# One hybrid decoder layer in a single instruction plan: norms kept per token, sums left in DRAM, another order of products and a plain opening of the first down projection

## The chip, the core and the metric

The kernel runs on one core of a Trainium2 chip. The metric is the device time of one execution in microseconds (us). A core has TensorE (PE, matmul, with a separate weight load PEld), VectorE (DVE), ScalarE (ACT), GpSimd (POOL) and SyncE (SP, which here only issues transfers), an on-chip SBUF of 128 partitions and a PSUM of eight banks, 128 x 512 fp32 each, into which PE writes.

## The reference

One layer on `x` of 1024 tokens by 1024 columns, and a last norm:

```python
def rms_norm(x, g):
    return x * lax.rsqrt(jnp.mean(x * x, -1, keepdims=True) + EPS) * g

mod = silu(c) @ mod_w + mod_b                      # 9 vectors of 1024
u = modulate(rms_norm(x, norm1_g), sh1, sc1)
x = x + 0.5 * g1 * swiglu(u, ffn1_w_up, ffn1_w_down)      # d_ff = 2816
u = modulate(rms_norm(x, norm2_g), sh2, sc2)
xa, ga, xb, mg_a, mg_b = split(u @ w_in + b_in)
ya = rg_lru(causal_depthwise_conv(xa)) * gelu(ga)
yb = gelu(s5_ssm(xb)); yb = yb * sigmoid(yb @ glu_w + glu_b)
m = sigmoid(mg_a) * (ya @ proj_a) + sigmoid(mg_b) * (yb @ proj_b)
x = x + g2 * (m @ w_out)
u = modulate(rms_norm(x, norm3_g), sh3, sc3)
x = x + 0.5 * g3 * swiglu(u, ffn2_w_up, ffn2_w_down)
out = rms_norm(x, final_g)
```

## The kernel before

Activations lie transposed: a tile has 128 columns of the model on its partitions and 512 tokens (half h = 0 or 1) along its rows, so x is 8 x 2 tiles. All arithmetic is fp32. A product of a 128 x 128 weight block with a tile is three matmuls in the chip's rounded fp32 form: weight and operand are each split into a rounded part (ACT, names `wh`, `act`) and a remainder (DVE, `wl`, `act`), and hi x hi, hi x lo and lo x hi are summed in a PSUM bank (`products`).

Two ways of multiplying are used. The *plain* way (`tile_of`) takes one output tile for both halves, k by k. The *paired* way (`pair`, `pair_weights`, `pair_operands*`) takes two output tiles, two halves and two halves of k as a 2 x 2 block problem and does it with seven products instead of eight, numbered 1 to 7. The weights of the products are sums of weight blocks, made by accumulating transfers that POOL issues (`plus`); the operands are sums and differences of tiles on DVE, each split again. Products 1, 2 and 3 use tiles of B as they are; 4 to 7 use sums. `pair_operands` makes them block by block of k, `pair_operands_by_product` in the order in which `pair` wants them (1, 6, 2, 7, 5, 4, 3). After products, `pair` adds banks together: a copy on ACT (`s1`) and six additions on DVE.

Nothing is issued as it is written. Every call is recorded in a `Plan`, which then sets the order on each engine: it walks a clock of its own with costs from `cost`, and takes on each engine the ready call of lowest number. `ahead` lowers the number (weights by 200, sums of pairs by 300, loads of gated tiles by 100). A tile needs a free slot of its tag (65 of `act`, 6 `tmp`, 8 `wh`, 8 `wl`, 4 `wr`, 8 banks); a call whose slot isn't free waits. All instructions therefore have one line (L437 before, L439 after), and tiles are told by name. Background work (modulation vectors, the set-up of S5, the scans) is spread between products by `spread` and `tick` at a rate per tick.

The order of the work: norm of x; up projection of FFN1 with SwiGLU, gated tiles to DRAM (`g_d`); its down projection in four blocks of k (6, 6, 6 and 4 tiles of 128), each plain or paired as `PARTS` says, the outputs being summed in 16 SBUF tiles of x; norm; `w_in`: S5 input first (`put_xb`, four plain tiles), then the gates ga and mg_a paired, then xa and mg_b plain, with S5 and the scans in the background; `proj_b`, `proj_a` (four pairs), `w_out`; norm; FFN2 in the same way, with its sums kept in DRAM; last norm in three pieces (512, 256 and 256 tokens).

A norm sums squares over columns, so over partitions: squares on ACT, added over the 8 tiles on DVE (or in PSUM, in the first norms), then a matmul with a 128 x 128 block of ones, which leaves the sum of each token in all 128 rows; square root on ACT, reciprocal on DVE, 128 x 512 each.

Of the kernel before, what the change touches and what calls it, by code (L numbers as in the profile page):

```python
# [46 lines left out]
SETUP_RATE, MOD_RATE, GAIN_RATE, LATE_RATE = 1.0, 0.18, 0.1, 0.2  # L47
# [7 lines left out]
    ((6, True), (6, False), (6, True), (4, False)),  # L55
# [18 lines left out]
class Plan:  # L74
# [130 lines left out]
    def cost(self, call, table):  # L205
        engine, method, args, kwargs = call
        out = args[0]
        n = 1
        for s in out.shape[1:]:
            n *= s  # L210
        psum = any(
            getattr(a, "space", None) == bass.MemoryType.PSUM for a in args[1:]
        )
        if engine == "tensor":
            rhs = kwargs.get("rhs", args[1] if len(args) > 1 else None)
            return max(60.0, n * 1.7 if rhs.dtype == F32 else (n + 32) / 2.4), table
# [13 lines left out]
        return 65 + n * (max(rate, 1.05) if psum else rate), table  # L230
# [211 lines left out]
class Layer:  # L442
# [175 lines left out]
    def pair_operands_by_product(self, b11, b21, b12, b22):  # L618

        nc = self.nc  # L620
        split = lambda ts: [self.split(t) for t in ts]
        xs = {1: split(b11)}
# [7 lines left out]
        xs[2] = split(b21)  # L630
# [7 lines left out]
        xs[3] = split(b22)  # L638
        return xs

    def pair(self, w, xs):
# [13 lines left out]
        self.tick()  # L655
        product(b, 6)
# [3 lines left out]
        product(a, 2, True)  # L660
        self.tick()
# [12 lines left out]
        product(c, 3, True)  # L674
# [29 lines left out]
    def square(self, st, x, d):  # L704
# [5 lines left out]
        if st[0] is None:  # L710
            st[0] = sq
        else:
            acc = self.act()[:, :n]
            nc.two(ALU.add, acc, st[0], sq)
            st[0] = acc

    def rstd(self, st):

        nc = self.nc
        n = st[0].shape[1]  # L720
        hi, lo = self.tmp(F32R)[:, :n], self.tmp(F32R)[:, :n]
        nc.scalar.activation(hi, st[0], AF.Copy)
        nc.vector.tensor_sub(lo, st[0], hi.bitcast(F32))
        ps = self.bank()[:, :n]
        self.mm(ps, self.ones, hi, True, False)
        self.mm(ps, self.ones, lo, False, True)
        return self.rstd_of(ps)

    def rstd_of(self, ps):
        nc = self.nc  # L730
        n = ps.shape[1]
        root = self.tmp()[:, :n]
        nc.scalar.activation(root, ps, AF.Sqrt, bias=self.eps, scale=1.0 / D)
        r = self.act()[:, :n]
        nc.vector.reciprocal(r, root)
        return r

    def modulate(self, x, r, l, d):

        nc = self.nc  # L740
        if r is not None:
            nc.two(ALU.mult, x, x, r)
# [58 lines left out]
    def up(self, w_up, u, t, f0, job=None):  # L801

        xs = self.pair_operands(
# [213 lines left out]
def s5_setup(L):  # L1017
# [5 lines left out]
    L.ident = L.con("ident", [P, P])  # L1023
    st = {}

    def params():
        softplus_scales(L)
        yield
        make_identity(L.tc.nc, L.ident)
# [217 lines left out]
class Mixer:  # L1247
# [19 lines left out]
    def put_xb(self, m, h, ps):  # L1267
# [4 lines left out]
            t.rearrange("p (j c) -> p c j", j=4), ps.rearrange("p (c j) -> p c j", j=4),  # L1272
# [222 lines left out]
    def run(self):  # L1495
# [4 lines left out]
        xs = L.pair_operands(  # L1500
# [7 lines left out]
        for dst, i0, fn in ((self.ga_d, 8, AF.Gelu_apprx_tanh), (self.mga_d, 20, AF.Sigmoid)):  # L1508
            for i in range(i0, i0 + 8, 2):
                c11, c12, c21, c22 = L.pair(  # L1510
                    L.pair_weights([io["w_in"][i], io["w_in"][i + 1]]), xs
# [38 lines left out]
        for p, pair in enumerate(PROJ_A):  # L1550
            c11, c12, c21, c22 = L.pair(L.pair_weights([io["proj_a"][d] for d in pair]), ya)
            for e, h, c in ((0, 0, c11), (1, 1, c22), (1, 0, c21), (0, 1, c12)):
                d = pair[e]
                t, r = self.load(self.mga_d, d, h), self.load(self.q_d, d, h)
                nc.vector.tensor_mul(t, t, c)
                nc.two(ALU.add, t, t, r)
                if p < M_OUT:
                    nc.sync.dma_start(self.m_d[d][:, h * H : (h + 1) * H], t)
                    with nc.ahead(GATED_AHEAD):
                        m[h][d] = self.load(self.m_d, d, h)  # L1560
                else:
                    m[h][d] = t
# [5 lines left out]
        st = [[None], [None]]  # L1568
        u3 = L.u3 = [[], []]

        def put(d, h, ps):
# [4 lines left out]
            L.square(st[h], t, d)  # L1576
            x[h][d] = self.load(L.x2_d, d, h) if d < W_PAIRED else t
            if d == ND - 1:
                s = L.rstd(st[h])
# [41 lines left out]
def hybrid_layer(ctx: ExitStack, tc: tile.TileContext, io):  # L1621
# [6 lines left out]
    L.ones = L.con("ones", [P, P], F32R)  # L1628
# [3 lines left out]
    nc.vector.memset(L.ones.bitcast(F32), 1.0)  # L1632
# [37 lines left out]
    def norm(h):  # L1670
        ps = L.bank()
        for d in range(ND):
            sq = L.act()
            nc.scalar.activation(sq, x[h][d], AF.Square)
            L.mm(ps, L.ones.bitcast(F32), sq, d == 0, d == ND - 1)
        r = L.rstd_of(ps)
        for d in range(ND):
            nc.two(ALU.mult, x[h][d], x[h][d], r)
# [48 lines left out]
    st = [[None], [None]]  # L1727
    u2 = [[], []]

    def on_x(d, h, x):  # L1730
        L.square(st[h], x[h][d], d)
        if d == ND - 1:
            r = L.rstd(st[h])
# [13 lines left out]
    st3 = [[None] for _ in pieces]  # L1747

    def on_out(d, p, x):
        h, c = pieces[p]  # L1750
        L.square(st3[p], x[h][d][:, c], d)
        if d == ND - 1:
# [4 lines left out]
            r = L.rstd(st3[p])  # L1757
            for e in range(ND):
                if e in scaled:
                    o = scaled[e]  # L1760
                    nc.gpsimd.tensor_mul(o, o, r)
# [109 lines left out]
```

## Time and profile before

| | |
|---|---|
| time, median of 3 runs | 2054.34 us (2054.18 to 2054.97) |
| the profiled execution | 2057.46 us, of which 2055.7 us are the span of the profile |
| PE busy | 1991.2 us, 97% of the span, 8866 matmul rows |
| DVE busy | 1554.1 us, 76% |
| ACT busy | 1065.2 us, 52% |
| POOL busy | 324.3 us, 16% |
| mean granted clock of TensorE | 0.987 of full speed |
| transfers | 393.06 MB, mean 191 GB/s |

The busy share is an average over stages. Rows of the views give start, duration, engine, line, operation, tile written <- tiles read, shape; a row of the timeline with x3 at its end stands for three instructions in a row, and the bracket says how long the engine had been idle before it, and what ended that. Matmul rows overlap, so distances between starts say more than durations.

### The profile page before, as it was taken

Reading aid. Unit: us, or ns where it says so; the run is one execution under the profiler, and the core shown is the slowest. Engines: PE = TensorE matmul, PEld = TensorE weight load, DVE = VectorE, ACT = ScalarE, POOL = GpSimd, SP = SyncE. Lnnn points to the kernel's source line nnn. Section 1 sums busy time; section 2 is a strip of 40 time slices with the busy share of each in tenths; the row PEclk is TensorE's granted clock in tenths of the full one; section 3 lists DMA queues with packets and bytes.
Section 4 is the critical chain, followed back from the end, with each engine's and each line's share of the span. In section 5 each row is a group of like instructions: output and inputs, shape, how many; then the busy total and the mean of one; then the engine's idle time right before and its main releaser. Section 6 shows DMA issues by size and latency. Waiting matters only on the chain. (4 is left out here: it accounts for less than half of the span.)

```text
span 2055.7 us, 27034 instructions
## 1 busy us (share of the span) xinstructions
PE 1991.2 (97%) x8866; PEld 1635.7 (80%) x8866; DVE 1554.1 (76%) x3064; ACT 1065.2 (52%) x1842; POOL 324.3 (16%) x409
## 2 busy tenths in 40 slices
PE   6999999998999999999999999899999999999997
PEld 3888888886888878788878888677888888887886
DVE  8997777778969787767999597879544444497757
ACT  5744344344434574455789643447443344366753
POOL 0222122121011001100000011100111121134442
PEclk9999999999999999999999999999999999999998
DMA  7767676778756367787555689662765565589993
GB/s 261 192 156 208 180 197 185 198 193 265 238 156 178 130 172 206 217 251 248 174 173 196 230 253 280 210 235 74 173 159 133 129 150 136 123 210 220 203 230 127
DMA packets 188045, 393.06 MB, mean 191 GB/s; under 512 B 20992, under 2 KB 44672, under 8 KB 187904
## 3 DMA queue, kind: packets, MB, share of 16 engines
q1 hardware_dynamic: 121504, 278.45, 40.8%
q0 software_dynamic: 49536, 84.96, 24.6%
q10 hardware_dynamic: 16864, 27.93, 3.7%
q8 instruction: 69, 1.13, 0.2%
q14 instruction: 72, 0.59, 0.1%
HBM read 262.81 MB, written 92.27 MB: 173 GB/s over the span
## 5 line engine op out<-in xcount | busy, mean ns | idle before, releaser
L437 PE MATMUL ps_in<-act_in,wh_in 128*128 128x512 f32 (+1 forms) x5592 | 1685.6, 390 | 37.3 <-ACT act_in L437 12.5
L437 PEld LDWEIGHTS ps_in<-act_in,wh_in 128*128 128x128 f32 x5592 | 1050.0, 189 | 263.5 <-DVE act_in L437 17.2
L437 PE MATMUL ps_in<-act_in,wl_in 128*128 128x512 f32 (+1 forms) x2796 | 1047.7, 389 | 0.0
L437 ACT ACTIVATE wh_in<-wr_in 128x512 fp32r<-128x512 f32 (+2 forms) x544 | 323.8, 601 | 571.6 <-PE ps_in L437 451.7
L437 PEld LDWEIGHTS ps_in<-act_in,wl_in 128*128 128x128 f32 x2796 | 528.6, 189 | 107.6
L437 DVE TENSOR_TENSOR wl_in<-wr_in,wh_in 128x512 fp32r<-128x512 f32 (+2 forms) x544 | 352.3, 653 | 174.3 <-ACT wh_in L437 173.1
L437 DVE TENSOR_TENSOR act_in<-act_in,act_in 128x512 f32<-128x512 f32 (+3 forms) x632 | 400.0, 677 | 30.9 <-ACT act_in L437 24.0
L437 DVE TENSOR_TENSOR tmp_in<-ps_in,tmp_in 128x512 f32<-128x512 f32 x296 | 203.9, 689 | 160.3 <-PE ps_in L437 157.0
L437 ACT ACTIVATE act_in<-act_in 128x512 fp32r<-128x512 f32 (+3 forms) x414 | 238.0, 612 | 129.6 <-DVE act_in L437 107.0
L437 POOL DMA_DIRECT2D wr_in<-wr_in x148 | 136.5, 922 | 544.9 <-ACT wr_in L437 169.8
L437 ACT ACTIVATE tmp_in<-ps_in 128x512 f32<-128x512 f32 x130 | 76.3, 589 | 51.9 <-PE ps_in L437 44.2
L437 POOL DMA_DIRECT2D re_in<-in_ffn_w_up x40 | 35.6, 890 | 426.0 <-ACT re_in L437 307.0
L437 ACT ACTIVATE wr_in<-wr_in 128x512 f32<-128x512 f32 (+1 forms) x148 | 85.2, 594 | 23.3 <-DVE wl_in L437 21.9
L437 DVE TENSOR_TENSOR tmp_in<-tmp_in,ps_in 128x512 f32<-128x512 f32 x82 | 56.0, 685 | 41.7 <-PE ps_in L437 41.1
L437 ACT ACTIVATE wh_in<-re_in 128x512 fp32r<-128x512 f32 (+1 forms) x74 | 44.3, 599 | 67.9 <-PE ps_in L437 65.2
L437 DVE SCALAR_TENSOR_TENSOR mw_in<-mw_in,cact 128x1024 f32<-128x1024 f32 x56 | 68.3, 1220 | 8.3 <-DMA mw_in<-in_mod_w 8.2
L437 DVE TENSOR_TENSOR tmp_in<-tmp_in,tmp_in 128x512 f32<-128x512 f32 (+1 forms) x96 | 66.0, 688 | 5.8 <-ACT tmp_in L437 5.2
L437 DVE SCALAR_TENSOR_TENSOR act_in<-ps_in,mods,act_in 128x512 f32<-128x512 f32 (+1 forms) x68 | 46.2, 686 | 29.1 <-PE ps_in L437 28.9
L437 PE MATMUL ps_in<-act_in,act_in 128*128 128x256 f32 (+1 forms) x336 | 57.8, 317 | 3.8 <-DVE act_in L437 2.3
L437 PEld LDWEIGHTS ps_in<-act_in,act_in 128*128 128x128 f32 x336 | 49.2, 190 | 12.5 <-DVE act_in L437 4.9
L437 POOL DMA_DIRECT2D x_d<-tmp_in x48 | 50.2, 1266 | 53.0 <-ACT tmp_in L437 51.5
L437 ACT ACT_TABLE_LOAD x42 | 53.9, 1283 | 2.4 <-PEq L1860 1.7
(109 smaller groups left out, 1019.4 us busy)
## 6 DMA issues: line engine op xcount, KB each, us to landing
wr_in<-in_ffn_w_up SPq DMA_DIRECT2D x84, 512.0 KB, 3.7
mw_in<-in_mod_w SPq DMA_DIRECT2D x56, 512.0 KB, 4.3
wr_in<-wr_in POOLq DMA_DIRECT2D x108, 256.0 KB, 5.1
g_d<-tmp_in SPq DMA_DIRECT2D x88, 256.0 KB, 4.0
act_in<-g_d SPq DMA_DIRECT2D x88, 256.0 KB, 6.0
wr_in<-in_ffn_w_down SPq DMA_DIRECT2D x48, 384.0 KB, 4.0
wr_in<-in_w_in SPq DMA_DIRECT2D x36, 512.0 KB, 3.9
x_d<-tmp_in POOLq DMA_DIRECT2D x48, 256.0 KB, 7.5
```

The source lines that it names most:

```text
L437: getattr(getattr(self.nc, engine), method)(*map(self.place, args), **{k: self.place(v) for k, v in kwargs.items()})
```

## The change

Seven edits, all in what is recorded; the order of everything is then set anew by the planner.

1. The two first norms and the three pieces of the last one keep the sum of a token on the token's own partition. For the last norm the squares are the weights of matmuls with two columns of ones (`square`), so that four (or two) blocks of 128 tokens give a tile of 128 x 8 (128 x 4); for the first norms the full sums are copied out of PSUM and brought into this form by four matmuls with two columns of an identity. Square root and reciprocal work on 128 x 8, and four (two) fp32 matmuls with the identity spread the result over 128 rows again, into PSUM, from where the multiplications read it (`rstd`). A square root of 128 x 2 at the first square of a piece (`early`) is there to set ACT's table. The norms of FFN1's output and of w_out's keep the old form (`rstd_rows`).
2. For the first two pairs of `proj_a` the gated product is added to `q_d` in DRAM by an accumulating transfer and read back, instead of being added on DVE, stored to `m_d` and read back.
3. In the first pair of gates the products go 1, 3, 2, 6, 7, 5, 4, with product 3 in a fifth bank and one more addition.
4. `up` (FFN1, FFN2) and the gates make their operands by product.
5. `put_xb` reads PSUM strided and writes in order, instead of the reverse.
6. FFN1's down projection is plain, paired, paired, plain instead of paired, plain, paired, plain.
7. Two background rates are lower, and the planner's cost of short fp32 matmuls is higher; the identity is made at the start.

The diff, cut to its core:

```diff
-SETUP_RATE, MOD_RATE, GAIN_RATE, LATE_RATE = 1.0, 0.18, 0.1, 0.2
+SETUP_RATE, MOD_RATE, GAIN_RATE, LATE_RATE = 1.0, 0.14, 0.1, 0.16
 PARTS = (
-    ((6, True), (6, False), (6, True), (4, False)),
+    ((6, False), (6, True), (6, True), (4, False)),
     ((6, True), (6, True), (6, True), (4, False)),
 )
-    def pair(self, w, xs):
+    def pair(self, w, xs, late=False):
...
+        if late:
+            e = self.bank()
+            product(e, 3)
+            product(a, 2, True)
+            self.tick()
         product(b, 6)
         with nc.ahead(SUMS_AHEAD):
             nc.vector.tensor_add(u2, b, s1)
         self.tick()
-        product(a, 2, True)
-        self.tick()
+        if late:
+            with nc.ahead(SUMS_AHEAD):
+                nc.vector.tensor_add(u2, e, u2)
+        else:
+            product(a, 2, True)
+            self.tick()
...
+    def rstd(self, ps, n):
+
+        nc = self.nc
+        k = n // P
+        r = self.con(self.name("rstd"), [P, 2 * k])
+        self.root(r, ps[:, : 2 * k])
+        nc.vector.reciprocal(r, r)
+        out = self.bank()[:, :n]
+        for b in range(k):
+            self.mm(
+                out[:, b * P : (b + 1) * P], r[:, 2 * b : 2 * b + 1].to_broadcast([P, P]),
+                self.ident, True, True,
+            )
+        return out
...
     def up(self, w_up, u, t, f0, job=None):
 
-        xs = self.pair_operands(
+        xs = self.pair_operands_by_product(
...
         nc.scalar.activation(
-            t.rearrange("p (j c) -> p c j", j=4), ps.rearrange("p (c j) -> p c j", j=4),
+            t.rearrange("p (j c) -> p j c", j=4), ps.rearrange("p (c j) -> p j c", j=4),
             AF.Identity, bias=L.col("b_in", 16 + m),
         )
...
-                t, r = self.load(self.mga_d, d, h), self.load(self.q_d, d, h)
+                t = self.load(self.mga_d, d, h)
                 nc.vector.tensor_mul(t, t, c)
-                nc.two(ALU.add, t, t, r)
                 if p < M_OUT:
-                    nc.sync.dma_start(self.m_d[d][:, h * H : (h + 1) * H], t)
+                    nc.plus(self.q_d[d][:, h * H : (h + 1) * H], t)
                     with nc.ahead(GATED_AHEAD):
-                        m[h][d] = self.load(self.m_d, d, h)
+                        m[h][d] = self.load(self.q_d, d, h)
                 else:
+                    r = self.load(self.q_d, d, h)
+                    nc.two(ALU.add, t, t, r)
                     m[h][d] = t
...
-        r = L.rstd_of(ps)
+        sums = L.tmp()
+        nc.scalar.activation(sums, ps, AF.Copy)
+        ps = L.bank()
+        for b in range(H // P):
+            L.mm(
+                ps[:, 2 * b : 2 * b + 2], sums[:, b * P : (b + 1) * P], L.ident[:, :2],
+                True, True,
+            )
+        r = L.rstd(ps, H)
         for d in range(ND):
-            nc.two(ALU.mult, x[h][d], x[h][d], r)
+            nc.vector.tensor_mul(x[h][d], x[h][d], r)
```

How the order moves, at three places. First PE where FFN1's down projection opens, before (product 1 of the paired block into `ps_983`, then product 6 into `ps_984`, which the order leaves after two of its three blocks of k):

```order
L437 MATMUL ps_983_in<-act_922_in,wh_969_in 128x512
L437 MATMUL ps_983_in<-act_923_in,wh_969_in 128x512
L437 MATMUL ps_983_in<-act_922_in,wl_970_in 128x512
L437 MATMUL ps_984_in<-act_930_in,wh_973_in 128x512
L437 MATMUL ps_984_in<-act_931_in,wh_973_in 128x512
L437 MATMUL ps_984_in<-act_930_in,wl_974_in 128x512
```

and the same place now (the last rows of the up projection, in `ps_896`, then the first plain tile, both halves of it in `ps_950` and `ps_951`):

```order
L439 MATMUL ps_896_in<-act_207_in,wh_892_in 128x512
L439 MATMUL ps_896_in<-act_206_in,wl_893_in 128x512
L439 MATMUL ps_950_in<-act_910_in,wh_946_in 128x512
L439 MATMUL ps_950_in<-act_911_in,wh_946_in 128x512
L439 MATMUL ps_951_in<-act_913_in,wh_946_in 128x512
L439 MATMUL ps_951_in<-act_914_in,wh_946_in 128x512
L439 MATMUL ps_950_in<-act_910_in,wl_947_in 128x512
```

Before, the block that opens is paired; now it is plain, and its first k is followed by the next k in the same two banks.

Second, DVE at the step from the second to the third block of FFN1's down projection, which are both paired now (the first row is the last sum of the second block; the `act` rows with `act` inputs are differences, or remainders of operands, of the third; `wl` are remainders of weights; the rows of act_1198, act_1200 and act_1202 are the remainders that product 6 waits for, those of act_1204, act_1206 and act_1208 those of product 2; `tmp_1255` is a sum after the third block's first product 6):

```order
L439 TENSOR_TENSOR tmp_1171_in<-ps_1168_in,tmp_1171_in 128x512
L439 TENSOR_TENSOR act_1196_in<-act_1193_in,act_1184_in 128x512
L439 TENSOR_TENSOR act_1198_in<-act_1194_in,act_1197_in 128x512
L439 TENSOR_TENSOR act_1200_in<-act_1195_in,act_1199_in 128x512
L439 TENSOR_TENSOR wl_1261_in<-wr_1257_in,wh_1260_in 128x384
L439 TENSOR_TENSOR act_1202_in<-act_1196_in,act_1201_in 128x512
L439 TENSOR_TENSOR act_1204_in<-act_1176_in,act_1203_in 128x512
L439 TENSOR_TENSOR wl_1249_in<-wr_1233_in,wh_1248_in 128x384
L439 TENSOR_TENSOR wl_1263_in<-wr_1257_in,wh_1262_in 128x384
L439 TENSOR_TENSOR tmp_1255_in<-ps_1251_in,tmp_1254_in 128x512
L439 TENSOR_TENSOR act_1206_in<-act_1177_in,act_1205_in 128x512
L439 TENSOR_TENSOR act_1208_in<-act_1178_in,act_1207_in 128x512
```

Before, a plain block stood between two paired ones; there is no such place in the order of before.

Third, DVE in the first norms, before (a remainder of the first operand, two modulation vectors, then the reciprocal of the second half and its first multiplications):

```order
L437 TENSOR_TENSOR act_131_in<-act_72_in,act_130_in 128x512
L437 SCALAR_TENSOR_TENSOR wr_132_in,mods<-wr_132_in,cact 128x1024
L437 SCALAR_TENSOR_TENSOR wr_133_in,mods<-wr_133_in,cact 128x1024
L437 TENSOR_TENSOR mods<-mods,cols 128x1
L437 RECIPROCAL act_146_in<-tmp_145_in 128x512
L437 SCALAR_TENSOR_TENSOR gsc<-mods,cols 128x1
L437 TENSOR_TENSOR mods<-mods,cols 128x1
L437 TENSOR_TENSOR act_122_in<-act_122_in,act_146_in 128x512
```

and now (the same remainder, the modulation vectors, then remainders of weights):

```order
L439 TENSOR_TENSOR act_138_in<-act_77_in,act_137_in 128x512
L439 SCALAR_TENSOR_TENSOR wr_139_in,mods<-wr_139_in,cact 128x1024
L439 SCALAR_TENSOR_TENSOR wr_140_in,mods<-wr_140_in,cact 128x1024
L439 TENSOR_TENSOR mods<-mods,cols 128x1
L439 TENSOR_TENSOR wl_95_in<-act_156_in,wh_94_in 128x256
L439 SCALAR_TENSOR_TENSOR gsc<-mods,cols 128x1
L439 TENSOR_TENSOR mods<-mods,cols 128x1
L439 TENSOR_TENSOR wl_99_in<-act_157_in,wh_98_in 128x256
L439 TENSOR_TENSOR wl_103_in<-act_158_in,wh_102_in 128x256
L439 TENSOR_TENSOR wl_107_in<-act_159_in,wh_106_in 128x256
L439 TENSOR_TENSOR wl_97_in<-act_178_in,wh_96_in 128x256
```

The reciprocal of the second half (128 x 8 now) stands 24 rows behind that remainder instead of four, after twelve remainders of weights and two more modulation vectors, and its eight multiplications follow three rows later.

## Rows read from the trace of the kernel before

**Rows 1.** The profile's page: span, busy time by engine, granted clock in 40 slices

```profile
span 2055.7 us, 27034 instructions
...
PE 1991.2 (97%) x8866; PEld 1635.7 (80%) x8866; DVE 1554.1 (76%) x3064; ACT 1065.2 (52%) x1842; POOL 324.3 (16%) x409
...
PEclk9999999999999999999999999999999999999998
```

**Rows 2.** Windows: length, then busy time of each engine (instructions), PEclk, DMA share, GB/s

```profile
480.00:510.00 30.00, 21.55 (x82) 16.44 (x82) 24.68 (x56) 9.39 (x20) 6.15 (x7) 0.83 0.98 295
...
510.00:520.00 10.00, 10.00 (x45) 8.10 (x44) 9.82 (x19) 4.16 (x9) 0.52 (x1) 1.00 0.26 67
...
750.00:770.00 20.00, 16.27 (x61) 12.93 (x60) 17.47 (x29) 15.64 (x26) 2.65 (x3) 0.83 0.84 255
...
1290.00:1320.00 30.00, 22.88 (x87) 17.26 (x86) 24.46 (x45) 9.93 (x17) 3.08 (x4) 0.89 0.61 194
...
1380.00:1400.00 20.00, 17.09 (x68) 13.49 (x67) 17.40 (x25) 16.00 (x26) 1.73 (x2) 0.91 0.42 132
```

**Rows 3.** Timelines, FFN1's down opening: PE, then ACT, then PE's short S5 rows

```profile
493.09 0.50 PE L437 MATMUL ps_in<-act_in,wh_in 128*128 128x512 f32 x1 [3.16 <-ACT act_in L437]
...
503.10 1.22 PE L437 MATMUL ps_in<-act_in,wh_in 128*128 128x512 f32 x2 [3.50 <-DVE tmp_in L437]
...
491.99 0.52 ACT L437 ACTIVATE wh_in<-wr_in 128x384 fp32r<-128x384 f32 x1 [5.81 <-DMA wr_in<-wr_in]
...
498.62 0.98 PE L437 MATMUL ps_in<-cb_in,act_in 128*128 128x32 f32 x8
```

**Rows 4.** Timeline of DVE, splits of m ahead of w_out

```profile
1298.91 5.50 DVE L437 TENSOR_TENSOR act_in<-act_in,act_in 128x512 fp32r<-128x512 f32 x9
```

**Rows 5.** Timelines, first gates: ACT (S5 input, copy of the sum), then PE

```profile
739.73 1.20 ACT L437 ACTIVATE tmp_in<-ps_in,cols 128x512 f32<-128x512 f32 x1
...
764.12 0.58 ACT L437 ACTIVATE tmp_in<-ps_in 128x512 f32<-128x512 f32 x1
...
764.75 1.22 PE L437 MATMUL ps_in<-act_in,wh_in 128*128 128x512 f32 x2 [3.73 <-ACT tmp_in L437]
```

**Rows 6.** Timelines, norm ahead of FFN2: DVE, PE, then ACT

```profile
1383.61 3.35 DVE L437 RECIPROCAL act_in<-tmp_in 128x512 f32<-128x512 f32 x1
...
1386.87 1.23 DVE L437 TENSOR_TENSOR wl_in<-wr_in,wh_in 128x512 fp32r<-128x512 f32 x2
...
1390.83 0.49 PE L437 MATMUL ps_in<-act_in,wh_in 128*128 128x512 f32 x1 [2.47 <-ACT act_in L437]
...
1380.35 1.28 ACT L437 ACT_TABLE_LOAD   x1
1381.64 0.69 ACT L437 ACTIVATE tmp_in<-ps_in,eps 128x512 f32<-128x512 f32 x1
```

**Rows 7.** Timelines, first norms: DVE, ACT, PE

```profile
18.86 3.35 DVE L437 RECIPROCAL act_in<-tmp_in 128x512 f32<-128x512 f32 x1
...
22.25 5.51 DVE L437 TENSOR_TENSOR act_in<-act_in,act_in 128x512 f32<-128x512 f32 x9
...
13.43 1.28 ACT L437 ACT_TABLE_LOAD   x1
...
35.59 0.79 PE L437 MATMUL ps_in<-act_in,wh_in 128*128 128x512 f32 x1 [5.00 <-ACT act_in L437]
```

**Rows 8.** Timelines, the end: PE, DVE

```profile
2045.89 0.58 PE L437 MATMUL ps_in<-tmp_in,ones 128*128 128x256 f32 x1 [0.42 <-DVE tmp_in L437]
...
2047.08 1.75 DVE L437 RECIPROCAL act_in<-tmp_in 128x256 f32<-128x256 f32 x1 [1.24 <-ACT tmp_in L437]
...
2048.87 3.56 DVE L437 SCALAR_TENSOR_TENSOR act_in<-act_in,cols,act_in 128x256 f32<-128x256 f32 x5
```

**Rows 9.** Groups of DVE by form, whole span: sums from PSUM, sums from SBUF

```profile
L437 DVE TENSOR_TENSOR tmp_in<-ps_in,tmp_in 128x512 f32<-128x512 f32 x296 | 203.9, 689 | 160.3 <-PE ps_in L437 157.0 <-DMA ga_d<-tmp_in 1.1 <-DMA x_d<-tmp_in 0.7
...
L437 DVE TENSOR_TENSOR act_in<-act_in,act_in 128x512 f32<-128x512 f32 x280 | 182.8, 686 | 17.0 <-ACT act_in L437 11.1 <-DMA act_in<-q_d 4.2 <-DMA act_in<-g_d 1.1
```

More of the change, by code (lines that the diff above doesn't have):

```diff
@@ L629, in pair_operands_by_product @@
         xs[6] = split(t2)
-        xs[2] = split(b21)
+        if not known:
+            xs[2] = split(b21)
         for r, v in zip(b12, b22):
@@ L673, in pair @@
         self.tick()
-        product(c, 3, True)
+        if not late:
+            product(c, 3, True)
         with nc.ahead(SUMS_AHEAD):
@@ L709, in square @@
         nc.scalar.activation(sq, x, AF.Square)
-        if st[0] is None:
-            st[0] = sq
-        else:
+        if d == 0:
+            st[:] = [sq, None]
+            self.root(self.con(self.name("early"), [P, 2]), sq[:, :2])
+            return
+        if rows or d < ND - 1:
             acc = self.act()[:, :n]
@@ L715, in square @@
             st[0] = acc
-    def rstd(self, st):
+        if rows:
+            return
+        if d == ND - 2:
+            hi, lo = self.tmp(F32R)[:, :n], self.tmp(F32R)[:, :n]
+            nc.scalar.activation(hi, acc, AF.Copy)
+            nc.vector.tensor_sub(lo, acc, hi.bitcast(F32))
+            st[1] = self.bank()
+            for b in range(n // P):
+                c = slice(b * P, (b + 1) * P)
+                out = st[1][:, 2 * b : 2 * b + 2]
+                self.mm(out, hi[:, c], self.ones, b == 0, False, b > 0)
+                self.mm(out, lo[:, c], self.ones, False, True, b > 0)
@@ L719, in rstd, with root, rstd_rows @@
+        if d == ND - 1:
+            for b in range(n // P):
+                self.mm(
+                    st[1][:, 2 * b : 2 * b + 2], sq[:, b * P : (b + 1) * P],
+                    self.ones.bitcast(F32), False, True, True,
+                )
+    def root(self, out, sums):
+        self.nc.scalar.activation(out, sums, AF.Sqrt, bias=self.eps, scale=1.0 / D)
+    def rstd_rows(self, st):
         nc = self.nc
-        n = st[0].shape[1]
-        hi, lo = self.tmp(F32R)[:, :n], self.tmp(F32R)[:, :n]
+        hi, lo = self.tmp(F32R), self.tmp(F32R)
@@ L722, in rstd @@
         nc.scalar.activation(hi, st[0], AF.Copy)
         nc.vector.tensor_sub(lo, st[0], hi.bitcast(F32))
[L724 to L734, printed above, removed]
+        ps = self.bank()
@@ L735, in rstd_of @@
+        self.mm(ps, self.ones_p, hi, True, False)
+        self.mm(ps, self.ones_p, lo, False, True)
+        root = self.tmp()
+        self.root(root, ps)
+        r = self.act()
         nc.vector.reciprocal(r, root)
         return r
+    def rstd(self, ps, n):
[6 more added lines that the diff above has]
+        for b in range(k):
+            self.mm(
+                out[:, b * P : (b + 1) * P], r[:, 2 * b : 2 * b + 1].to_broadcast([P, P]),
+                self.ident, True, True,
+            )
+        return out
@@ L1627, in hybrid_layer @@
     L.gsc = L.con("gsc", [P, 24])
-    L.ones = L.con("ones", [P, P], F32R)
+    L.ones_p = L.con("ones_p", [P, P], F32R)
+    ones = L.ones_p.bitcast(F32)
+    L.ones = L.ones_p[:, :2]
+    L.ident = L.con("ident", [P, P])
+    make_identity(tc.nc, L.ident)
     L.eps = L.con("eps", [P, 1])
@@ L1756, in on_out @@
                 nc.scalar.activation(scaled[e], x[h][e][:, c], AF.Copy, scale=L.col("final_g", e))
-            r = L.rstd(st3[p])
+            r = L.rstd(st3[p][1], c.stop - c.start)
+            if scaled:
+                r_copy = L.act()[:, : c.stop - c.start]
+                nc.scalar.activation(r_copy, r, AF.Copy)
             for e in range(ND):
```

44 lines of the change are left out of this document (24 added, 20 removed).

## Prediction, made before the changed kernel was run

> **What bounds the kernel now.** The page comes first: PE is busy for 1991.2 us of a span of 2055.7 us, and the granted clock is 9 tenths or more in 39 of 40 slices [rows 1]. No other engine comes near, so the time is the products plus the places where PE stands still or runs slowly. The change leaves the number of products as it is; what it can win are those places, about 65 us in all, and the windows say where they are [rows 2]. A full stretch of 10 us holds 45 matmul rows (510 to 520 us). By that measure 480 to 510 us has 82 rows, of which 12 are short ones of S5 that take 1.3 us, so 30 - 70/4.5 - 1.3 = 13 us are lost; 750 to 770 us loses 20 - 61/4.5 = 6.4; 1290 to 1320 us loses 30 - 87/4.5 = 10.7; 1380 to 1400 us loses 20 - 68/4.5 = 4.9. [...] The reader then asks the timelines what PE waited for in each. Besides these four there are the start and the end, where 9 us of the span lie behind the last matmul row (2045.89 + 0.58) [rows 8].
>
> **1. FFN1's down opens plain.** PE waits 3.16 us for ACT and 3.50 us for DVE there, and ACT itself stood 5.81 us on an accumulating transfer of weights [rows 3], with the DMA engines at 0.98 [rows 2]. A paired opening needs seven sums of operands and POOL's sums of weights at once; a plain one needs twelve splits and one plain weight. In the order of now all twelve remainders stand on DVE ahead of the last sum of the up projection, so they cost nothing; the cover is that last pair, and without it they would be 12 x 0.60 = 7 us. (0.60 is the distance of nine DVE operations in a row, 5.50 us, less the overhang [rows 4].) I keep 0.5 us of the 13.
> What is late next: the second and the third block are both paired now. The third needs 12 differences and 21 remainders on DVE, 33 x 0.60 = 19.8 us, and before, a plain block with little for DVE to do lay ahead of it. Now x holds 16 tiles and the running block's operands 42, so of 65 slots seven are left, and the order starts on the third block's operands only when the last pair of the second gives tiles back. I walked DVE's order there by hand with 0.60 us per 512 columns and 0.47 per 384: from the second block's last sum, 0.25 us after its last product, product 6 finds its remainders 0.2 us late, product 7 2.2 us, product 4 0.55 us, as the order fills the gaps with the next pair's products. That is 3 us, and 3.5 with some slow clock. The ends are 0, as FFN1's other paired block showed under its plain one, and 19.8, if nothing is covered; the walk decides. Term: 13 to 0.5 + 3.5, **-9**.
>
> **2. First gates.** PE waited 3.73 us for ACT's copy of the first product's sum [rows 5]. That copy ran 0.58 us but came late, behind splits and the S5 input, whose eight strided writes take 1.20 us each. Now products 3 and 2 stand between product 1 and product 6, all three on tiles that exist: 2 x 12 x 0.227 = 5.4 us in which the copy may be late. put_xb's cost falls to about that 0.58 plus a bias, so ACT gets 8 x 0.5 = 4 us back. The added addition is 0.69 us of DVE. Ends: 0 and 6.4; nearest to the wait that goes, with half of the slow clock: **-5**. By-product operands in `up` and here are the same instructions in another order; in `up` DVE's backlog covers them either way: 0.
>
> **3. Sums in DRAM.** For two of four pairs, eight additions leave DVE (4.8 us), eight stores and as many loads leave SP's queue, and eight accumulating transfers go to POOL, which is busy for 3.08 us of 30 there [rows 2]. Nothing waits for them soon: the tiles belong to the first two pairs, two pairs of products ahead of `w_out`. Where `w_out` opens, DVE works without a gap on splits of m [rows 4]. From the sum after product 4 of the last pair to the last remainder that `w_out` needs I count 28 rows of the order before and 23 now: 16.4 against 13.8 us. Ends: a loss of 5, if the read-back comes late, and a gain of 8; the count decides: **-3**.
>
> **4. The norm ahead of FFN2** keeps its form, but moves: the reciprocal of 3.35 us was followed by 1.23 us of weight remainders before the first multiplication [rows 6], and it had waited behind an addition that itself waited for PE. In the order of now it follows the sums at once and its multiplications follow it at once. PE's wait of 2.47 us shrinks by that 1.2 and by some of what the addition cost, and with it the slow clock of this stretch. Ends -1 and -4.9: **-3**.
>
> **5. The first norms.** A reciprocal of 3.35 us and the root ahead of it [rows 7] become a copy out of PSUM (0.6), eight short fp32 matmuls, a root and a reciprocal of 128 x 8 (some 0.4 together) and four matmuls that spread the result, about 2.8 instead of 4.0 us: the first half's result comes 1.2 to 1.5 us earlier. ACT's table load (1.28 [rows 7]) moves behind that copy, but beside the matmuls. DVE is full here, though, and its order decides: by the same prices as above, the first remainder of the second half stands 13.6 us of DVE work behind that of the first half in the order of before (a reciprocal of 3.35 between), and 17.4 us now, behind twelve remainders of weights, four modulation vectors of 1.20 and eight multiplications. So it comes 3.8 - 1.5 = 2.3 us later. PE already stood still for 5.00 us in this place [rows 7], and stands longer; the weights of the next steps are ready sooner, which gives a little back. Ends -1 and +4: **+2**.
> Elsewhere the row of a root starts 1.29 us after its table load did, which lasted 1.28 [rows 6]: nothing lies between. [...]
>
> **6. The end.** Before: 1.75 us of reciprocal and 3.56 us of multiplications on DVE [rows 8]. Now a reciprocal of 128 x 4, two short matmuls with the identity, and multiplications that read PSUM, at 0.40 us apart; some 3.5 us less behind the last product. But PE gets about 24 short rows for the first piece and 12 for the second, 0.11 us each by the S5 rows (0.98 for eight [rows 3]), less the matmuls with ones that go: +3. **-1**, with ends -4 and +2.
> Reading PSUM is costed at nothing: DVE sums from PSUM take 689 ns, from SBUF 686 [rows 9]. [...]
>
> **7. Rates and planner costs.** The number of modulation vectors stays. The last of FFN1's run under the plain block, which has room on DVE. The stretches not named above, S5 and the scans with them, are ordered anew; no row names a sign: 0, with ends -3 and +3, a little under the smallest of the four losses.
>
> Sum: -9 - 5 - 3 - 3 + 2 - 1 = **-19 us**. On the profiled execution (2057.46 us) this gives 2038.5; it lay 3.1 us above the median, so against the median of 2054.34 it gives **2035.3 us**.
>
> **The rivals.**
> - *The stall only moves.* What the opening of FFN1's down loses turns up again between its second and third block. For: only seven free slots. Against: the walk. The 9 us of term 1 go: 2044.3.
> - *The waits go with all their slow clock.* Terms 2 to 4 win 6.4, 8 and 4.9: -27, so 2027. For: the clock column of every such stretch [rows 2]. Against: `w_out`'s DVE still has 13.8 us to do.
> - *Only term 1 is real.* The planner fills its time elsewhere: -9 + 2, 2047.
> - *It doesn't do what it says.* Every stretch finds another stall; 2053.
> - *Slower.* One mechanism: operands made by product hold more tiles at once, so they run out of slots, and DVE's work for a block's operands lies open instead of under products. Two places: the third block's 33 rows (19.8 us) and the gates' 32 (12 differences, four additions, 16 remainders: 19.2 us). All open, that costs 39 us where the two places lose 19.4 today: +19.6 + 2 - 7 = +14.6, so 2069. It decides from 73% open on. For: the gates' stretch has DVE at 17.5 of 20 us [rows 2]. Against: the order starts the gates' operands under plain tiles.
>
> **How the numbers follow.** Forecast 0.40, stall moves 0.18, all waits go 0.18, only term 1 0.11, nothing 0.07, slower 0.06. The forecast's own range, with the ends of its terms taken as independent, is 2027 to 2044. From 2024 (all waits go, and 3 us of the new order) to 2051 leaves out the last two cases and a little of the edges, 2 in 10. A measurement can tell about 0.2%, 4.1 us, from no change: faster is below 2050.2, which takes the first four cases, 0.86 of 0.87; same 0.07; slower 0.07.
>
> **What would show it.** In the profile of the changed kernel: 480 to 510 us with 110 matmul rows or more and a clock near 1; some 130 us later, at the second paired-to-paired step, PE waits for DVE `act` of 2 to 4 us in sum; the PE wait for ACT's `tmp` copy at the first gates gone; the reciprocal ahead of FFN2 directly followed by multiplications; a longer idle of PE than 5.00 us in the first norms; behind the last product 6 us instead of 9. Wrong I would be by waits of over 8 us at the paired-to-paired step, by a wait for `q_d` ahead of `w_out`, or by new waits in the gates for operands.

## The result

In the same comparison the kernel before took 2054.26 us (median of 4) and the changed kernel **2031.64 us** (2029.34 to 2032.96): a ratio of 0.9888, interval 0.9871 to 0.9906, 22.6 us less. I had said 2035.3, 19 us less, in a range of 2024 to 2051. The number held. The account behind it did not: what I gave the largest price wins nothing that the runs can tell beside the other parts, and what I costed at 0 wins, put in alone, two thirds as much as the whole change. How that shows is what the experiments are for.

The profile after, on an execution of 2032.34 us. First the page, against [rows 1]:

```profile
span 2030.5 us, 27147 instructions
...
PE 1989.4 (98%) x8940; PEld 1638.2 (81%) x8940; DVE 1536.1 (76%) x3054; ACT 1067.8 (53%) x1855; POOL 330.6 (16%) x417
...
PEclk8999999999999999999999999999999999999999
```

PE is busy for nearly as long as before (1.8 us less, with 74 short rows more), and the span is 25.1 us shorter. So it is mostly standing still that went: 64.5 us of the span before, 41.1 now. The windows, for the stretches of [rows 2] at the times that they have now, with the step between the two paired blocks (600 to 615 us) added:

```profile
480.00:510.00 30.00, 30.00 (x134) 24.86 (x133) 18.43 (x33) 9.22 (x18) 3.52 (x4) 1.00 0.86 286
...
600.00:615.00 15.00, 13.13 (x56) 10.02 (x55) 15.00 (x28) 8.95 (x19) 3.52 (x4) 1.00 0.55 112
750.00:770.00 20.00, 16.92 (x70) 12.85 (x69) 14.60 (x25) 12.40 (x22) 3.52 (x4) 0.91 0.82 198
1275.00:1305.00 30.00, 27.36 (x114) 21.84 (x113) 28.15 (x49) 13.11 (x21) 3.51 (x4) 0.94 0.66 203
1365.00:1385.00 20.00, 19.12 (x81) 14.73 (x80) 17.32 (x26) 14.74 (x25) 1.72 (x2) 1.00 0.44 123
```

Each of the four stretches that the prediction priced has more matmul rows and a higher granted clock than in [rows 2]. PE's timeline shows which waits are there now (start, between the paired blocks, first gates, `w_out`, end):

```profile
40.36 0.79 PE L439 MATMUL ps_in<-act_in,wh_in 128*128 128x512 f32 x1 [2.85 <-ACT act_in L439]
43.08 0.80 PE L439 MATMUL ps_in<-act_in,wh_in 128*128 128x512 f32 x1 [1.92 <-DVE act_in L439]
...
610.38 0.50 PE L439 MATMUL ps_in<-act_in,wh_in 128*128 128x512 f32 x1 [1.58 <-DVE act_in L439]
...
752.14 0.73 PE L439 MATMUL ps_in<-act_in,wh_in 128*128 128x512 f32 x2 [0.96 <-ACT wh_in L439]
754.65 0.50 PE L439 MATMUL ps_in<-act_in,wl_in 128*128 128x512 f32 x1 [1.77 <-DVE wl_in L439]
...
1286.32 0.50 PE L439 MATMUL ps_in<-act_in,wh_in 128*128 128x512 f32 x1 [1.65 <-DVE act_in L439]
...
2023.10 0.68 PE L439 MATMUL ps_in<-ident,rstd 128*128 128x128 f32 x4 [0.66 <-DVE rstd L439]
```

To place the gain, number the 8388 matmuls in each trace that read a weight tile, and compare when the nth starts; between two of them the difference is what that stretch won or lost (these are the numbered products below, and "the 100th product" is the 100th of these matmuls). "After" is the changed kernel:

| stretch | predicted, us | after minus before, us |
|---|---|---|
| start to FFN1's end (S5 setup beside it) | +2 | +4.7 |
| FFN1's down, opening | -12.5 | -14.5, and -0.85 behind it |
| between the two paired blocks | +3.5 | +2.7 |
| first gates | -5 | -0.6 |
| S5 and LRU beside the products | 0 | -4.0 |
| proj_a and the opening of `w_out` | -3 | -5.8 |
| norm ahead of FFN2 | -3 | -2.9 |
| opening of FFN2's down (code unchanged) | 0 | -3.1 |
| behind it, the end included | -1 | -0.9 |

The table makes the opening of FFN1's down look right to 2 us. A place is not a cause, though: it says where the time went, not which line of the diff sent it.

A place can also be an accident of the one execution that was profiled. The changed kernel and e11 below have the same order on every engine from end to end, and e11's edit acts from about 730 us on; yet ahead of it their traces already differ by 1.0 us at the 100th product and by 1.4 between the two paired blocks (+2.7 and +4.1). From 680 us on the kernel before and e1 have the same order too, on PE, DVE, ACT and POOL, and yet e1's trace is 4.5 us shorter near 868 us and 2.2 shorter at the opening of FFN2's down. So differences of about 1.5 us at one place say little, and at these two places the profiled execution of the kernel before (3.2 us above its median) has losses that other executions of the same order do not have.

### The profile page after: what moved, and what is told of

It reads as the page before. It is cut to its first block, busy times and chain, and to the rows that moved or that the text cites. A ratio compares the mean times of both kernels' runs of the same rounds, so it can differ in the third digit from the quotient of the medians.

```text
span 2030.5 us, 27147 instructions
## 1 busy us (share of the span) xinstructions
PE 1989.4 (98%) x8940; PEld 1638.2 (81%) x8940; DVE 1536.1 (76%) x3054; ACT 1067.8 (53%) x1855; POOL 330.6 (16%) x417
## 4 chain that ended last, share of the span: by engine, by line
PE 70%; DVE 8%; issue 8%; DMA 8%; ACT 4%; POOL 1%; SPq 0%; POOLq 0%; ACTq 0%; DVEq 0%
PE ps_in L439 70%; DVE act_in L439 3%; DMA wr_in<-wr_in 3%; ACT act_in L439 3%; DVE tmp_in L439 2%; DVE wl_in L439 2%; DVE mw_in L439 1%; ACT tmp_in L439 1%; DMA wr_in<-in_w_in 1%; ACT wh_in L439 1%; DMA act_in<-g_d 1%; DVE sd_in L439 0%; DMA x_d<-tmp_in 0%; DMA act_in<-u_d 0%; DMA wr_in<-in_ffn_w_up 0%
## 5 line engine op out<-in xcount | busy, mean ns | idle before, releaser
L439 PEld LDWEIGHTS ps_in<-act_in,wh_in 128*128 128x128 f32 x5592 | 1045.4, 188 | 237.9 <-DVE act_in L439 10.6
L439 DVE TENSOR_TENSOR act_in<-act_in,act_in 128x512 fp32r<-128x512 f32 (+3 forms) x611 | 386.7, 677 | 26.9 <-ACT act_in L439 25.0
```

What stands on the lines that cost most here:

```text
L439: getattr(getattr(self.nc, engine), method)(*map(self.place, args), **{k: self.place(v) for k, v in kwargs.items()})
```

## Experiments

All ratios are to the kernel before, measured beside each run (its medians there were 2053.8 to 2055.2). A trace is one execution: those of e4, e5, e7 and e10 ran 3.1 to 3.7 us above the median of their kernel, that of e1 3.0 below it. So a kernel's time is taken from the medians, and traces are used for places and waits.

| run | median, us | ratio, interval |
|---|---|---|
| changed kernel | 2031.64 | 0.9888 (0.9871 to 0.9906) |
| e1 opening alone | 2050.07 | 0.9981 (0.9971 to 0.9992) |
| e2 opening undone | 2029.34 | 0.9876 (0.9863 to 0.9890) |
| e3 late order undone | 2031.14 | 0.9886 (0.9871 to 0.9902) |
| e4 old first norms | 2030.31 | 0.9886 (0.9873 to 0.9900) |
| e5 rates alone | 2038.69 | 0.9926 (0.9914 to 0.9938) |
| e6 opening and rates undone | 2049.37 | 0.9976 (0.9967 to 0.9985) |
| e7 sums undone | 2036.71 | 0.9915 (0.9902 to 0.9928) |
| e8 opening undone, old first norms | 2030.43 | 0.9882 (0.9865 to 0.9899) |
| e9 first rate alone | 2044.02 | 0.9948 (0.9935 to 0.9960) |
| e10 rates half way | 2041.10 | 0.9925 (0.9911 to 0.9938) |
| e11 old write of the S5 input | 2032.88 | 0.9892 (0.9875 to 0.9909) |
| e12 opening undone, old gate operands | 2025.78 | 0.9856 (0.9842 to 0.9871) |

### e1 and e2: the opening, alone and undone

```
 e1: before.py, and in e2 the other way round
-    ((6, True), (6, False), (6, True), (4, False)),
+    ((6, False), (6, True), (6, True), (4, False)),
```

> The kernel before with one line of the change: FFN1's down opens with a plain block and has its second block paired. Theory (the parts add up, and the opening is the largest): the two waits of 3.16 and 3.50 us and the accumulating transfer ahead of them go, about 2.8 us of waits appear between the second and the third block as in the changed kernel, 2054.3 - 12.5 = 2042, give or take 2. Rival (the opening's gain hangs on the other parts, because the modulation vectors and the planner's costs decide what DVE does under the plain block): 2047 to 2050, with over 5 us of waits between the second and the third block.

> The changed kernel with the old parts of FFN1's down: paired, plain, paired, plain. Theory (the parts add up): 2031.6 + 12.5 = 2044, with two waits of 3 us or more at about 495 to 510 us. Rival (the other parts would have softened the old opening too): 2036 to 2040, with one such wait or none.

Both theories fell, and e2 lies below the range of its rival too. Alone, the line is worth some 4 us: the opening is as clean as in the changed kernel, but between the two paired blocks most of it comes back. Windows of e1 at the opening, then at that step:

```profile
480.00:510.00 30.00, 30.00 (x139) 24.93 (x138) 15.97 (x35) 7.73 (x16) 3.54 (x4) 1.00 0.81 272
590.00:620.00 30.00, 24.99 (x92) 18.68 (x91) 26.48 (x50) 13.89 (x28) 4.86 (x6) 0.89 0.68 171
```

By the numbered products it wins 14.5 us at the first place and loses 9.5 at the second: two thirds of the gain go the way of the prediction's rival "the stall only moves". And with the paired opening put back into the changed kernel (e2) PE hardly waits there:

```profile
480.00:510.00 30.00, 29.82 (x128) 23.43 (x127) 29.88 (x55) 15.34 (x32) 6.97 (x8) 1.00 1.04 317
```

Compare 82 rows at a clock of 0.83 for the same code in [rows 2]. So another part of the change mends the paired opening, and with that part in place the plain one wins nothing that can be told: e2's median is 2.3 us lower than the changed kernel's, and the intervals of the two ratios overlap.

### e5, e6, e9, e10: the rates

Which part can it be? The planner's orders, without a run, narrow it down. Put back one at a time in e2, the old operands of `up` and of the gates, the order of the first gates' products and the early root leave the order of DVE, ACT and POOL at the opening as it is, row by row. The rates, the planner's costs and the first norms change it. So the rates alone, and the rates undone:

```
 e5: before.py (e9: 0.14, 0.2; e10: 0.16, 0.18); e6: changed kernel, old parts and old rates
-SETUP_RATE, MOD_RATE, GAIN_RATE, LATE_RATE = 1.0, 0.18, 0.1, 0.2
+SETUP_RATE, MOD_RATE, GAIN_RATE, LATE_RATE = 1.0, 0.14, 0.1, 0.16
```

> The kernel before with nothing but the two rates changed (modulation vectors at 0.14 and 0.16 instead of 0.18 and 0.2); FFN1's down still opens paired. Theory (the rates move the vectors, whose transfers of 512 KB and 1.7 us of DVE stood at 480 to 482 us beside the opening's sums, and so take the opening's waits away): the waits of 3.16 and 3.50 us and ACT's 5.81 us on an accumulating transfer go, and the time is 2042 to 2046. Rival (the planner's new costs of short matmuls did it): both waits stay, 2052 to 2056.

> The changed kernel with the old parts of FFN1's down and the old rates; the new costs stay. Theory (the rates heal the paired opening): beside the 2029.3 us of the run with the old parts alone, some 10 us come back at 480 to 510 us, 2038 to 2041. Rival (the costs do): no wait above 1 us there, 2028 to 2032.

The rates won by more than was expected, in e5 and in e6: two numbers take 15.1 us off the kernel before (0.9926), and taking them back in e2 costs 20 us. The windows at the opening, e5 and then e6, and the wait that PE has there in e6, with the one of ACT ahead of it:

```profile
480.00:510.00 30.00, 28.80 (x118) 21.03 (x117) 29.11 (x52) 14.63 (x31) 6.87 (x8) 1.00 1.02 296
```

```profile
480.00:510.00 30.00, 21.78 (x84) 16.87 (x83) 25.36 (x52) 11.82 (x24) 6.09 (x8) 0.83 0.77 236
```

```profile
493.27 0.52 ACT L439 ACTIVATE wh_in<-wr_in 128x384 fp32r<-128x384 f32 x1 [5.09 <-DMA wr_in<-wr_in]
...
493.85 1.22 PE L439 MATMUL ps_in<-act_in,wh_in 128*128 128x512 f32 x2 [7.58 <-ACT wh_in L439]
```

By the numbered products, e5 wins 11.2 us at 480 to 510 us and loses 3.2 ahead of it, beside the S5 setup; most of the rest comes between 860 and 1010 us. e6 loses 10.6 at the opening and 9 to 10 between 930 and 1130 us.

> The kernel before with the first rate alone (0.14 for the vectors made during FFN1); the second stays at 0.2. Theory (each rate acts on the stretch that its vectors lie in): the 11 us at 480 to 510 us are won, the 5 us between 860 and 1010 us are not, 2043 to 2045. Rival (what was won between 860 and 1010 us also came with the new order ahead of it): 2038 to 2040, as with both rates.

> The kernel before with the rates half way, 0.16 and 0.18. Theory (fewer vectors beside the products, less lost: the time goes with the rate): between the two, 2044 to 2049. Rival (the rates act only by where single vectors and loads happen to fall, so that a value between is no value in the middle): under 2041 or over 2052.

e9's time is what the theory says, its trace only half so: the opening gains 11.9 us, but 4.3 of what was put down to the second rate come too, since a wait of 2.69 us for a sum, near 868 us in the kernel before, is 0.5 us or less in e1, e5 and e9 alike (in e10 it is 2.39). e1 and e9 have the order of the kernel before at that place, so these 4 us are no gain of a rate. e10 speaks for accident and against a price per rate: half the step wins as much as the whole (0.9925 against 0.9926), though its median lies 0.1 us above the range that the rival named.

My own reason for the rates fell here as well. In e10 a modulation vector stands on DVE at 478 us, as one did at 480 us before, and PE waits little all the same (1.71 us between 480 and 510 us, 8.45 before). What differs by more is the chain that makes the weights' sums. SyncE's loads of `w_down` near the opening, before and then e5:

```profile
468.64 0.33 SPq L437 DMA_DIRECT2D wr_in<-in_ffn_w_down  x1
...
479.54 0.33 SPq L437 DMA_DIRECT2D wr_in<-in_ffn_w_down  x1
...
487.51 0.33 SPq L437 DMA_DIRECT2D wr_in<-in_ffn_w_down  x1
```

```profile
472.26 0.33 SPq L437 DMA_DIRECT2D wr_in<-in_ffn_w_down  x1
...
478.69 0.33 SPq L437 DMA_DIRECT2D wr_in<-in_ffn_w_down  x1
...
491.55 0.33 SPq L437 DMA_DIRECT2D wr_in<-in_ffn_w_down  x1
```

A load waits for a buffer that a remainder on DVE gives back (19.8 us in five waits between 440 and 510 us in the kernel before), POOL's accumulating transfers wait for the load (7.6 us in e2) and for each other (14.2 us in three waits in the kernel before), ACT for those (5.81 us [rows 3]), and PE for ACT (7.58 us in e6). In e5 ACT still waits, but for 3.49 us, and PE has other products:

```profile
491.57 0.52 ACT L437 ACTIVATE wh_in<-wr_in 128x384 fp32r<-128x384 f32 x1 [3.49 <-DMA wr_in<-wr_in]
```

In the slow orders PE ends up behind one such transfer (in e6, and at the first of its two long waits in the kernel before); which row of the order does it was not singled out and stays open.

Taken out together, opening and rates (e6) cost 17.7 us against the changed kernel, and the sums of e7 below cost 5.1: these parts cover the gain of 22.6 within the scatter of the runs. Two runs are missing, though. No run has the plain opening with the old rates in the changed kernel, so what the rates are worth beside it is open; opening and rates clear the same stall, and their gains do not add. And none has the planner's new costs alone. What mends the step between the two paired blocks, 9.5 us in e1 and 2.7 to 4.5 in the five runs that have it with the new rates, is not singled out either.

### e3 and e11: the order of products, and the S5 input

```
 e3
-                    L.pair_weights([io["w_in"][i], io["w_in"][i + 1]]), xs, i == 8
+                    L.pair_weights([io["w_in"][i], io["w_in"][i + 1]]), xs
 e11
-            t.rearrange("p (j c) -> p j c", j=4), ps.rearrange("p (c j) -> p j c", j=4),
+            t.rearrange("p (j c) -> p c j", j=4), ps.rearrange("p (c j) -> p c j", j=4),
```

> The changed kernel with the first gates' pair in the order of the others: product 6 right behind product 1. Theory (the order of products is what took the wait for ACT's copy away): PE waits 3 to 4 us for tmp at about 756 us, and 2033 to 2035. Rival (the cheaper write of the S5 input had already freed ACT, and products 3 and 2 taken early only called for their weights' remainders sooner): no wait for tmp above 1 us, the waits of 1.12 and 1.94 us for wh and wl go, and 2029 to 2031.6.

> The changed kernel with the S5 input written strided by ACT again (eight writes of 1.20 us). Theory (4 us more of ACT, but products 3 and 2 of the first gates' pair still stand between the copy and its user): no wait for tmp above 1 us at 750 to 765 us, 2031 to 2033. Rival (the copy gets so late that the order of products no longer covers it): a wait of 2 us or more for tmp or wh there, 2034 to 2036.

In each the time goes with one side and the trace with the other. PE at the first gates, e3 and then e11:

```profile
760.47 1.22 PE L439 MATMUL ps_in<-act_in,wh_in 128*128 128x512 f32 x2 [3.34 <-ACT tmp_in L439]
```

```profile
755.99 0.73 PE L439 MATMUL ps_in<-act_in,wh_in 128*128 128x512 f32 x2 [3.94 <-ACT wh_in L439]
758.02 0.79 PE L439 MATMUL ps_in<-act_in,wl_in 128*128 128x512 f32 x1 [1.29 <-DVE wl_in L439]
```

Without the late order the wait for ACT's copy is back (3.73 in [rows 5]) and the two waits for weights' splits are gone; about the same is lost either way, and the medians differ by 0.5 us. With the old write ACT is later by what it costs, and its next user, the weight split, makes PE wait 3 us longer; of the 3.4 us lost there 1.5 are left at the end. The write itself does what was said, 0.67 to 0.69 us instead of 1.20; in the changed kernel:

```profile
742.47 0.67 ACT L439 ACTIVATE tmp_in<-ps_in,cols 128x512 f32<-128x512 f32 x1
```

### e12: the gates' operands

```
-        xs = L.pair_operands_by_product(
+        xs = L.pair_operands(
             t[0][:4], t[0][4:], t[1][:4], t[1][4:], {1: u[0][:4], 2: u[0][4:], 3: u[1][4:]}
```

> The changed kernel with the old parts of FFN1's down, and the first gates' operands made row by row again; their first pair still takes products 3 and 2 early. Theory (operands by product put 32 operations of DVE in front of the second pair's weights, which is why PE waits 1.21 us for wh, 1.95 for wl and 1.52 for tmp there): two of the three go, 2 to 4 us less than the 2029.3 of the run with the old parts, 2025.5 to 2027.5. Rival (row by row, product 7 or 5 finds its last operand late instead): a new wait for act of 2 us or more at 755 to 775 us, 2029 to 2033.

The theory held; one wait is left where e2 had three:

```profile
751.92 0.73 PE L439 MATMUL ps_in<-act_in,wh_in 128*128 128x512 f32 x2 [1.38 <-ACT tmp_in L439]
```

3.8 us are won at this place, close to the 3.6 by which the medians of e2 and e12 differ. The trace has another 2.5 us ahead of it, but up to 738 us the two orders are the same, so those are no gain of the edit. At 2025.78 us, 0.9856, this is the lowest median of the study: e2 and the old operands at one place. Its interval ends where the changed kernel's begins, at 0.9871, and overlaps e2's.

### e7: the sums in DRAM

```
-                t = self.load(self.mga_d, d, h)
+                t, r = self.load(self.mga_d, d, h), self.load(self.q_d, d, h)
                 nc.vector.tensor_mul(t, t, c)
+                nc.two(ALU.add, t, t, r)
                 if p < M_OUT:
-                    nc.plus(self.q_d[d][:, h * H : (h + 1) * H], t)
+                    nc.sync.dma_start(self.m_d[d][:, h * H : (h + 1) * H], t)
...
```

> The changed kernel with the sums of the first two pairs of proj_a on DVE again, stored and loaded back. Theory (eight additions less on DVE and 16 transfers less on the queue of SyncE are what shortened the stretch up to w_out): 3 to 6 us more between 1270 and 1325 us, 2034.5 to 2037.5. Rival (the stretch was won by the order that the planner found for it, with or without the additions): under 1.5 us more in that stretch, 2030 to 2033.

The theory held: 5.1 us more in the median, 6.1 by the opening of `w_out`. Windows of the changed kernel and of e7:

```profile
1270.00:1320.00 50.00, 47.36 (x202) 38.41 (x201) 46.74 (x79) 27.27 (x48) 5.23 (x6) 0.97 0.71 211
```

```profile
1270.00:1320.00 50.00, 43.66 (x176) 34.54 (x175) 41.05 (x71) 24.86 (x43) 5.21 (x6) 0.93 0.68 212
```

26 matmul rows less; in this window PE stands still for 6.3 us in e7 and for 2.6 in the changed kernel. Of the parts that were run by themselves, this is the one whose sign, place and cause came out as argued.

### e4 and e8: the first norms

```
-        sums = L.tmp()
-        nc.scalar.activation(sums, ps, AF.Copy)
...
-        r = L.rstd(ps, H)
+        root = L.tmp()
+        L.root(root, ps)
+        r = L.act()
+        nc.vector.reciprocal(r, root)
...
-            nc.vector.tensor_mul(x[h][d], x[h][d], r)
+            nc.two(ALU.mult, x[h][d], x[h][d], r)
```

> The changed kernel with the first two norms as before: matmuls with ones, a root and a reciprocal of 128x512, and the multiplications free to go to GpSimd. Theory (the transposed norms put the second half's remainders later, behind 17.4 instead of 13.6 us of DVE work): the 3.5 to 4.7 us that the changed kernel lost up to the end of FFN1's up come back, 2027 to 2028. Rival (the loss at the start is the planner's new costs and the early root, not the norms): 2031 to 2033, and PE's wait for DVE act at about 40 us stays at 2 us or more.

> The changed kernel with the old parts of FFN1's down and the old first two norms. Theory (the start is 4 us shorter with the old norms, and what ate that in the run before this, one wait of 2.27 us at 375 us and what followed it, was an accident of the order): 2025 to 2026. Rival (a planner that orders everything anew gives a gain of the start back somewhere later, whatever the place): 2028 to 2031.

The transposed norms do cost 3.5 us by the 60th product and 4.3 by the 500th, as the theory says of the start; yet e4 ends 1.3 us earlier at most, within the intervals and between the two ranges expected, and e8 no earlier than e2. In e4 PE's timeline has, 340 us later:

```profile
375.02 0.73 PE L439 MATMUL ps_in<-act_in,wh_in 128*128 128x512 f32 x2 [2.11 <-DVE tmp_in L439]
```

A sum stands behind S5 setup on DVE there. Between the 500th and the 1500th product e4 gives back 3.5 us, e8 3.4, and e8 another 2.2 at the opening. I had called that an accident of e4; it came twice, and e5, which has the old norms and the new rates, loses 2.3 in the same stretch against the kernel before, where e1, with the old of both, loses 0.2. So with the new rates what the old norms win at the start is lost again beside S5 setup.

## Why the prediction was right, and where it was wrong

- **Term 7, rates and planner costs at 0, between -3 and +3: the step that failed.** I looked for a row that names a sign, found none, and took the absence for 0. The two rates alone are -15 (e5). The bound, "a little under the smallest of the four losses", had no reason behind it: the rates shift what stands on every queue at every later place, so its bound is the sum of all the losses.
- **Term 1, the opening, -9.** Place right (no wait left; +2.7 at the next step for 3.5, with waits of 0.19 and 1.58 us, a little under the 2 to 4 named), cause wrong. The line alone gives 4 us (e1), and none that can be told beside the other parts (e2). I read 13 us of stall as the price of a paired opening; it was the price of one order of it.
- **Term 2, first gates, -5.** The wait for the copy went, and PE waited for weights' splits in its place: -0.6. "By-product operands cost 0" failed here: undoing them wins the 3.8 us (e12). The list of what is late next stopped at the operands and left out the second pair's weights, which share DVE with them.
- **Term 3, -3:** right in mechanism, 5 to 6 in size (e7). The count of 16.4 against 13.8 us of DVE is near the 3.7 us of standing still between the two windows of e7. It left out the slow clock behind the waits, 0.93 against 0.97 there: the 26 rows are worth 5.9 us at 0.227 each, and the remaining 2.2 us are put down to it (an estimate from these figures).
- **Term 4, -3:** the stretch gave -2.9. The reciprocal at 1364.10 us is followed by one remainder of 0.63, then by the first multiplication, where 1.23 stood [rows 6]; this part was not run by itself. DVE there now:

```profile
1364.10 3.35 DVE L439 RECIPROCAL act_in<-tmp_in 128x512 f32<-128x512 f32 x1 [1.14 <-ACT tmp_in L439]
1367.37 0.63 DVE L439 TENSOR_TENSOR wl_in<-wr_in,wh_in 128x512 fp32r<-128x512 f32 x1
1367.91 0.68 DVE L439 TENSOR_TENSOR act_in<-act_in,act_in 128x512 f32<-128x512 f32 x1
```

- **Term 5, +2:** the direction was right, +4.7 at its place, but as two waits of 2.85 and 1.92 us behind short rows and not as one longer than 5.00. Yet the end is no later for it (e4).
- **Term 6, -1:** from the last product of weights to the end of the span it is 10.3 us where it was 14.7 (the last matmul rows begin 7.4 us before the end now, 9.8 before [rows 8]), and the short rows ahead of that product cost 3.5; -0.9.
- **Unforeseen:** FFN2's opening, whose code is as before, is 3.1 us shorter in the trace. Little of that need be the change's: e1, e5, e9 and e10, whose order on PE, DVE and ACT is there that of the kernel before, are 0.5 to 2.6 us shorter at it too.
- **The clock.** Behind the pauses of 3.16, 3.50, 3.73 and 2.47 us [rows 3, 5, 6] the products start 0.427 us apart, where a full stretch has 0.227. It is not so behind each pause: behind waits of 2.11 us (1297.24 us) and 1.44 us (1303.86 us) in the kernel before, and behind the 1.58 us between the paired blocks now, the next products start 0.23 apart after a first distance of 0.33 or 0.34. That the slow clock goes with the pause, of which terms 1, 2 and 4 count a part, was an assumption of mine, and no run shows what it is worth by itself; the trace shows granted clocks of 0.83, 0.83, 0.89 and 0.91 in the four stretches before [rows 2], and of 1.00, 0.91, 0.94 and 1.00 now.

Of the rivals, "the stall only moves" is what e1 does to two thirds, and "only term 1 is real" is refuted by e7. That the sum came near is luck in good part: the rates' gain lies where I had put term 1's, and the gates' missing 4.4 us were made up, in this trace, by S5 (-4.0) and FFN2 (-3.1), both costed at 0 and both at places where the profiled execution of the kernel before has losses of its own.

## What to carry to other kernels

When a planner orders all engines at once, a stall's place does not name its cause: undo the suspected line in the changed kernel as well as trying it alone, since here one of the two says -4 us and the other nothing that can be told (2.3 us the other way). Price a change of the planner's parameters not at 0 but by all the stalls of the kernel, and try them by themselves first: two numbers won alone two thirds as much as this whole change. Before a place in a trace is put down to an edit, look whether the order there changed at all: where it did not, the difference is that of two executions. And ask of each cleared wait what stands on that engine for the product after next.

## What the runs showed of the hardware

The table load of the square root stands in the first norms between ACT's copy and its root, in the changed kernel:

```profile
16.83 0.60 ACT L439 ACTIVATE tmp_in<-ps_in 128x512 f32<-128x512 f32 x1 [3.29 <-PE ps_in L439]
17.45 1.28 ACT L439 ACT_TABLE_LOAD   x1
18.74 0.27 ACT L439 ACTIVATE rstd<-ps_in,eps 128x8 f32<-128x8 f32 x1
```

It starts 0.02 us behind the copy's end and lasts 1.28 us, and the root starts 1.29 us behind the load's start; no other row of ACT lies between the three. The 16 multiplications on DVE that read PSUM in the first norms stand in a group of 36 whose mean is 682 ns (the 20 others stood there before):

```profile
L439 DVE TENSOR_TENSOR act_in<-act_in,ps_in 128x512 f32<-128x512 f32 x36 | 22.8, 682 | 3.5 <-PE ps_in L439 3.2
```

Sums from SBUF take 686 [rows 9]: at 512 columns these 36, which read PSUM, took no longer.
